# Vector c kept in place, rotated keys in common buffers, column sums at other rates, squares on VectorE in a one-core decoder block

## The chip, the cores and the metric

The kernel runs on one core of a Trainium2 chip. A core has TensorE (matmuls), VectorE, ScalarE and GpSimd, and SyncE, whose queue here only issues DMAs. In the profile they are called PE (and PEld for its weight loads), DVE, ACT, POOL and SP. The metric is the device time of one execution in microseconds; lower is better.

## The reference

One layer of a decoder on a sequence of 512 tokens, in float32, width 2048. All of it is conditioned on one vector `c`:

```python
c_act = silu(c)
sh_a, sc_a, gt_a, sh_f, sc_f, gt_f = split(c_act @ w_ada + b_ada, 6)
h = rmsnorm(x, norm_mix) * (1 + sc_a) + sh_a
p = h @ w_in            # c_q, c_kv, k_pe, q, k, v, z, b, a, gate logits
y_a = mla(c_q, c_kv, k_pe) @ w_o_mla      # 8 heads, causal softmax, rotary part of 64
y_b = gated_delta_net(q, k, v, z, b, a) @ w_o_gdn
g_a, g_b = split(sigmoid(gate_logits), 2)
x = x + gt_a * ((g_a * y_a + g_b * y_b) @ w_o)
h = rmsnorm(x, norm_ffn) * (1 + sc_f) + sh_f
gate, up = split(h @ w_gate_up, 2)
x = x + gt_f * ((silu(gate) * up) @ w_down)
return rmsnorm(x, final_norm)
```

The two places that the change touches are the product `c_act @ w_ada` (six chunks of 2048 columns) and, in `rmsnorm(x, norm_ffn)`, the sum of the squares of `x` over the 2048 features of each token. The rotary keys `k_pe` after their rotation are the third thing that is moved.

## The kernel before

**Matmuls.** Every large product is taken in three matmuls: an operand is split into a rounded part `hi` (a cast on ScalarE) and a remainder `lo` (a subtraction on VectorE, both in `halves`, lines 263 and 264, or in `hilo`, lines 239 and 240), and hi·hi, hi·lo and lo·hi are added in PSUM.

**Order of the work.** A `Unit` is one piece of a weight matrix: `load` issues its DMA on SyncE, `split` makes `hi` and `lo`, `mms` is its list of matmuls (24 for most), and `pre` and `post` run before and after them. The `Driver` keeps up to `LOADS` = 4 units loaded and `AHEAD` = 2 units split ahead of TensorE. After every `GROUP` = 12 matmuls it takes one step of each side chain (`pump`); the chains are Python generators that write out the delta net, the attention, the normalisations and so on, a few instructions to a step. The scheduler of the framework then orders each engine's instructions; those of SyncE, GpSimd and TensorE stay in the order of the program (`PINNED`), as do single instructions that are marked, column sums among them.

**Main units.** `mixing()` yields them in this order, numbered here by their index in `mixed`: one that loads scalars (0), `ga8` and `ga12` (1 to 16), the sets `q03`, `k03`, `v03` (to 40), `kb` (to 44), `gb0`, `gb1` (to 60), `q47` (to 68), `k47` (to 76), `v47` (to 84), `z0`, `cq`, `ckv`, `z1` (to 116), six units for the rotary queries and the values (to 122), the eight heads' `qk` (to 130), `gb2` and `gb3` (16 each, to 162: eight units with matmuls, and between them eight that only reload pieces of the normalised input, `hh` and `hl`, or copy `x`), `ya` (to 182), `yb` (to 202). Then come `wo0` to `wo2` in a Strassen scheme and `wo3` in two halves of 256 tokens. The head, before them, runs `s1` and takes the column sums of chunk 1. The attention is a side chain that runs beside `qk`, `gb2` and `gb3`: at step i it takes the values of tile i-3, the transposes of i-2, the softmax of i-1 and the scores of i.

**Extra units.** `mixed` slips units of a second list, `extras()`, between the main units: `plan(i)` of them after main unit i. They have no matmuls. In `mod_units` one of them loads 512 KB of `w_ada` and takes a column sum on VectorE (`mod_sum`, line 435): the product with `silu(c)`, spread over all partitions as the tile `cbc`, and its sum in one instruction. A chunk has 32 of them. In `ada_units` one loads 512 KB of `w_in` and adds two scaled rows into `acc`. The order of the list is: chunk 0, 3, 2, 4 (`gt_mix`), four times eight `ada_units`, chunk 5 (`gt_ffn`).

**Buffers.** The pool `slots` has 68 common buffers of 128 x 512; `raws` has five of 512 KB for loaded weights, main units' and column sums' alike; the pool `wides` has a single one of 1 MB. The last holds `cbc` first, then `kp`, the rotated keys' `hi` and `lo` (of which it uses half), then `cbc` again, read back from `c_dram` once the attention has ended, and at last `euvw` of the Strassen stages.

**Squares.** `squares(q, seg, eng)` takes the squares of one tile on ScalarE and adds them to a running sum on the engine `eng`. For `q` 4 to 7 that is VectorE; for `q` 0 to 3 they are added on GpSimd in the chain `wo_rest`, which also fetches these tiles back from `x2_dram` and the pieces `a21` for the second half of `wo3`. `part_rstd` sums over the features with the matmuls `hss`; `spread` makes `hbc`, the inverse root spread over the partitions; `h2_gen(h)` then makes the normalised input of the feed-forward part (`h2f`, `h2T`) for one half of the tokens. `gu0` and `gu1` consume it.

Of the kernel before, what the change touches and what calls it, by code (L numbers as in the profile page):

```python
# [8 lines left out]
F32 = mybir.dt.float32  # L9
# [162 lines left out]
def block_kernel(ctx: ExitStack, tc: tile.TileContext, a: dict, out, out_t):  # L172
# [26 lines left out]
    def load(dst, src):  # L199
        nc.sync.dma_start(dst, src)  # L200
# [200 lines left out]

    c_dram = dram.tile([1, 4, 512], F32, name="c_dram")
    cbc = []

    def spread_c_again():
        cbc[0] = wides.tile([P, 4, 512], F32, tag="wide", name="cbc2")
        load(cbc[0][:].rearrange("p j n -> p (j n)"), c_dram.rearrange("o j n -> o (j n)").partition_broadcast(P))


    def spread_c():
        cbc.append(wides.tile([P, 4, 512], F32, tag="wide", name="cbc"))
        row = S("crow")
        load(row[0:P:32, :], a["c"].rearrange("o (j n) -> (o j) n", j=4))
        for j in range(4):
            ps = PS("cb")
            r = slice(32 * j, 32 * j + 1)
            mm(ps[:], ones[r, :], row[r, :], start=True, stop=True)
            nc.scalar.activation(cbc[0][:, j, :], ps[:], AF.Silu)  # L420
        side(c_dram, cbc[0][0:1])

# [584 lines left out]
    def rope_tables():  # L1009
        invf, posi = C("invf", [P, 32]), C("posi", [P, NT], I32)  # L1010
        side(invf[:], a["inv_freq"].partition_broadcast(P).rearrange("p o h -> p (o h)"))
        side(posi[:], a["positions"].rearrange("o (t p) -> p (o t)", p=P))
        yield 2
        posf = C("posf", [P, NT])
        nc.vector.tensor_copy(posf[:], posi[:])
        tmp = S("rt")[:].rearrange("p (a t e) -> p a t e", a=4, t=NT)
        ang, n, t1, t2 = (tmp[:, i] for i in range(4))
        for t in range(NT):
            nc.vector.tensor_scalar(ang[:, t, :], invf[:], posf[:, t:t + 1], None, op0=ALU.mult)
        nc.vector.tensor_scalar(n[:], ang[:], 0.15915494309189535, None, op0=ALU.mult)  # L1020
        nc.vector.tensor_scalar(n[:], n[:], 12582912.0, -12582912.0, op0=ALU.add, op1=ALU.add)
        for part in (6.28125, 0.0019350051879882812, 3.019916050195388e-07, 2.3999e-13):
            nc.vector.scalar_tensor_tensor(ang[:], n[:], -part, ang[:], op0=ALU.mult, op1=ALU.add)
        lim = 3.1415925
        nc.vector.tensor_scalar(ang[:], ang[:], lim, -lim, op0=ALU.min, op1=ALU.max)
        nc.scalar.activation(sin_[:], ang[:], AF.Sin)
        nc.scalar.activation(cos_[:], ang[:], AF.Sin, scale=0.5)
        nc.vector.tensor_tensor(cos_[:], cos_[:], cos_[:], ALU.mult)
        nc.vector.tensor_scalar(cos_[:], cos_[:], -2.0, 1.0, op0=ALU.mult, op1=ALU.add)
        kr = S("kr")[:].rearrange("p (t e) -> p t e", t=NT)  # L1030
        yield 2
        rope(kr[:, :, 0:64], kpe[:], NT, sin_[:], cos_[:], (t1, t2))
        nc.scalar.copy(kr[:, :, 64:128], kr[:, :, 0:64])
        yield 14
        kp = wides.tile([P, 4, 512], F32R, tag="wide", name="kp")
        ps = PS("kpT")
        for t in range(NT):
            nc.tensor.transpose(ps[:, tok(t)], kr[:, t, :], ident)
        hi, lo = (kp[:, i, :] for i in range(2))
        nc.scalar.copy(hi, ps[:])  # L1040
        nc.vector.tensor_tensor(lo, ps[:], hi.bitcast(F32), ALU.subtract)
        kpT.extend((hi, lo))

    w_uq, w_ukv = a["w_uq"][0], a["w_ukv"][0]
# [97 lines left out]
    def attention():  # L1142
        items = [(h, qb) for h in range(8) for qb in range(4)]
        n = len(items)
        box = [dict() for _ in items]
        yps = {}

        def scores(i):
            h, qb = items[i]
            N = max(qb + 1, 2) * P  # L1150
            ps = PS("sc")
            for q, k in ((0, 0), (0, 1), (1, 0)):
                mm(ps[:, 0:N], QN[h][q][:, tok(qb)], KN[h][k][:, 0:N], start=q == k, stop=False)
            for k in range(2):
                mm(ps[:, 0:N], qpT[h][:, tok(qb)], kpT[k][:, 0:N], start=False, stop=k == 1)
            box[i]["ps"] = ps
            if qb == 3:
                del QN[h], KN[h]

        def softmax(i):  # L1160
            h, qb = items[i]
            N = (qb + 1) * P
            ps = box[i].pop("ps")
            m, s, r = (sm[:, i, j:j + 1] for j in range(3))
            nc.vector.tensor_tensor(ps[:, tok(qb)], ps[:, tok(qb)], neg, ALU.add)
            nc.vector.tensor_reduce(m, ps[:, 0:N], AX.X, ALU.max)
            nc.vector.tensor_scalar(m, m, -scale, None, op0=ALU.mult)
            p = S("P")
            nc.scalar.activation(p[:, 0:N], ps[:, 0:N], AF.Exp, bias=m, scale=scale, accum_out=s)
            nc.vector.reciprocal(r, s)  # L1170
            nc.vector.tensor_scalar(p[:, 0:N], p[:, 0:N], r, None, op0=ALU.mult)
            box[i]["p"] = p

        def transposes(i):
            h, qb = items[i]
            N = (qb + 1) * P
            p = box[i].pop("p")
            ps = PS("pT")
            for kb in range(qb + 1):
                nc.tensor.transpose(ps[:, tok(kb)], p[:, tok(kb)], ident)  # L1180
            s = S("pT")
            (nc.scalar.copy if i % 2 else nc.vector.tensor_copy)(s[:, 0:N], ps[:, 0:N])
            box[i]["pT"] = s

        def values(i):
            h, qb = items[i]
            s = box[i].pop("pT")
            if qb == 0:
                yps[h] = PS("yT")
            for kb in range(qb + 1):  # L1190
                mm(yps[h][:, tok(qb)], V[h // 4][kb][:, tok(h % 4)], s[:, tok(kb)], start=kb == 0, stop=kb == qb)
            if qb == 3:
                yT[h] = hilo(yps.pop(h)[:], "y")
                if h % 4 == 3:
                    del V[h // 4]

        for i in range(n + 3):
            if i < n:
                while items[i][0] not in QN or items[i][0] not in qpT:
                    yield  # L1200
                if i == 0:
                    yield 2
            if i >= 3:
                values(i - 3)
            if 2 <= i < n + 2:
                transposes(i - 2)
            if 1 <= i < n + 1:
                softmax(i - 1)
            if i < n:
                scores(i)  # L1210
            yield
# [99 lines left out]
    def strassen_wo(n):  # L1311
# [20 lines left out]
        def freed(i):  # L1332
            if n == 2:
                wo_x["x56"][i] = wo_x["x73"][i] = None
                if i == 5:
                    for q in (4, 5):
# [4 lines left out]
                        [(c, i, j, lambda k, c=c: [wo_part(c, k, xi) for xi in range(2)]) for c, i, j in PRODUCTS],  # L1341
                        wo_ready, outputs, freed)

    def wo_rest():

        def squared(h):
            for q in range(4):
                squares(q, HALF[h], nc.gpsimd)
                yield

        for h in range(2):
            for q in range(4):
                x2[h][q] = S("x2")
                side(x2[h][q][:], x2_dram[h, q])
                yield
            if h == 0:
                for n in range(4):
                    t = S("a21")
                    load(t[:], a21_dram[n])
                    if n % 2:  # L1360
                        yield
                    a21[n] = t
                yield from squared(0)
                for n in range(4):
                    a21[n] = hilo(a21[n][:], "a21")
                    yield
        yield from squared(1)

    oT = [None] * 8

# [132 lines left out]
    def extras():  # L1503
# [29 lines left out]
        yield from mod_units(3, lambda ks: mod_columns(s_ffn, ks, b_cols[:, SC_F // P:SC_F // P + 16], n_ffn))  # L1533

        yield from mod_units(2, lambda ks: mod_columns(sh_ffn, ks, b_cols[:, SH_F // P:SH_F // P + 16]))
        yield from gate_units(4, gt_mix, GT_A)
        for n in range(4):
            yield from ada_units(w_in, sh_mix, O_GA + 512 * n, cols_done(n))
        while "att" not in chains or chains["att"] in drv.chains:
            yield Unit()  # L1540
        yield act(spread_c_again)
        yield from gate_units(5, gt_ffn, GT_F)

    known = set()

    def plan(i):
        return 2.0 if i < 16 else 0.85 if i < 48 else 1.2

    def act(fn):
        return Unit(load=fn)  # L1550
# [46 lines left out]
    def mixing():  # L1597
# [106 lines left out]
            chains["rest"] = drv.add(wo_rest())  # L1704
        with_pre(first, last)

        def rest():
            drv.finish(chains["rest"])
        yield from first + with_pre(with_pre(second, start_h2(0)), rest)


    def half_of(tile_, k):
# [488 lines left out]
    def ffn():  # L2201
        def gu0():
# [18 lines left out]
            def start():  # L2221
                for c in wo_x:
                    wo_x[c][:] = [None] * 8
                a21[:] = [None] * 4
                start_h2(1)()
            with_pre(us[0], start)
            return us[0] + us[1]
# [276 lines left out]
```

## Time and profile before

| | |
|---|---|
| median of 3 runs | 2752.79 us (2750.74 to 2755.06) |
| profiled execution | 2757.86 us |
| its span in the trace | 2756.1 us |
| TensorE, matmuls | busy 2716.6 us (99%) |
| TensorE, weight loads | busy 2357.8 us (86%) |
| VectorE | busy 2101.9 us (76%) |
| ScalarE | busy 1206.6 us (44%) |
| GpSimd | busy 273.8 us (10%) |
| DMA | 563.25 MB, 204 GB/s on average |
| granted clock of TensorE | 0.995 on average |

The profiled execution is one run apart from the three timed ones. The span is what the trace covers; the device time holds 1.8 us more around it. All matmuls stand under line 155, the call behind which the wrapper hides every TensorE and GpSimd instruction, so they are told apart by the names of their tiles. A matmul's busy time overlaps that of the next, because they are pipelined.

### The profile page before, as it was taken

To read this page: it belongs to the slowest core of one execution; us is meant where nothing else is said; L and a number is where in the kernel's file an instruction comes from. 1 tells how busy PE (TensorE), PEld (TensorE's weight loads), DVE (VectorE), ACT (ScalarE), POOL (GpSimd) and SP (SyncE) were. 2 spreads that over 40 slices of the span, in tenths; PEclk is the share of its full clock that TensorE was granted. 3 is DMA by queue.
4 is the path that set the end of the run, shared out by engine and by line. 5 is a ranking of instruction groups with operands and counts; after the bars stand their busy time and mean duration, and the time that the engine had idled before them with its cause. 6 is when DMAs were issued, how large, how long until landed. Compare 5 with 4: busy or idle time off the path is not lost.

```text
span 2756.1 us, 41080 instructions
## 1 busy us (share of the span) xinstructions
PE 2716.6 (99%) x15292; PEld 2357.8 (86%) x15292; DVE 2101.9 (76%) x3348; ACT 1206.6 (44%) x1715; POOL 273.8 (10%) x370
## 2 busy tenths in 40 slices
PE   9999999999999999999999999999999999999998
PEld 7888788788888888889999888888888888998997
DVE  8786666777887556788787877778778777878866
ACT  3443432442254343234473444444444445446545
POOL 0000011102001000001200000000000103113113
PEclk9999999999999999999999999999999999999999
DMA  9897566656675638725764556665665668568565
GB/s 361 302 350 268 182 195 194 214 162 212 202 213 184 209 132 303 264 76 132 263 184 141 194 200 199 202 218 199 203 202 194 218 202 196 122 196 203 131 184 168
DMA packets 315520, 563.25 MB, mean 204 GB/s; under 512 B 40788, under 2 KB 120820, under 8 KB 315192
## 3 DMA queue, kind: packets, MB, share of 16 engines
q1 hardware_dynamic: 264776, 460.04, 50.9%
q0 software_dynamic: 31904, 74.77, 10.6%
q10 hardware_dynamic: 18640, 25.83, 2.6%
q8 instruction: 119, 1.95, 0.3%
q14 instruction: 81, 0.66, 0.1%
HBM read 477.67 MB, written 83.90 MB: 204 GB/s over the span
## 4 chain that ended last, share of the span: by engine, by line
PE 83%; DVE 7%; DMA 5%; issue 2%; ACT 2%; SPq 0%; ACTq 0%; POOL 0%; DVEq 0%; POOLq 0%
PE m L155 41%; PE gb L155 6%; PE v L155 4%; PE gu L155 3%; PE ya L155 3%; PE dn L155 3%; PE yb L155 3%; PE s L155 3%; PE z L155 3%; DMA raw<-in_w_in_dram 2%; PE k L155 2%; PE q L155 2%; PE wo L155 1%; DVE rawm L435 1%; PE qk L155 1%
## 5 line engine op out<-in xcount | busy, mean ns | idle before, releaser
L263 ACT CAST hi<-raw 128x1024 fp32r<-128x1024 f32 x250 | 259.7, 1040 | 560.3 <-DMA raw<-in_w_in_dram 220.4
L264 DVE TENSOR_TENSOR lo<-raw,hi 128x1024 fp32r<-128x1024 f32 x250 | 305.4, 1223 | 198.5 <-ACT hi L263 181.1
L1831 ACT CAST hi<-raws 128x512 fp32r<-128x512 f32 (+1 forms) x240 | 218.6, 911 | 327.5 <-PE m L155 264.0
L1832 DVE TENSOR_TENSOR lo<-raws,hi 128x512 fp32r<-128x512 f32 (+1 forms) x240 | 247.4, 1042 | 87.8 <-ACT hi L1831 87.6
L155 PE MATMUL m<-xl,hi 128*128 128x256 f32 x1088 | 309.7, 285 | 3.9 <-DVE xl L240 3.9
L155 PE MATMUL m<-xh,hi 128*128 128x256 f32 x1088 | 309.5, 284 | 3.9 <-ACT xh L239 2.3
L155 PE MATMUL m<-xh,lo 128*128 128x256 f32 x1088 | 309.4, 284 | 1.3 <-DVE lo L2007 1.3
L435 DVE CUSTOM_DVE_ANT_0 rawm<-rawm,cbc 128x1024 f32<-128x1024 f32 x192 | 234.2, 1237 | 8.6 <-DMA rawm<-in_w_mod_dram 8.3
L155 PEld LDWEIGHTS m<-xl,hi 128*128 128x128 f32 x1088 | 210.3, 193 | 4.8 <-DVE xl L240 4.7
L155 PEld LDWEIGHTS m<-xh,hi 128*128 128x128 f32 x1088 | 210.2, 193 | 4.6 <-ACT xh L239 2.7
L155 PEld LDWEIGHTS m<-xh,lo 128*128 128x128 f32 x1088 | 210.2, 193 | 1.7 <-DVE lo L2007 1.7
L155 PE MATMUL m<-hi,h2h 128*128 128x512 f32 x480 | 190.2, 396 | 0.4 <-DVE euvw L1849 0.4
L155 PE MATMUL m<-hi,h2l 128*128 128x512 f32 x480 | 187.2, 390 | 0.0
L155 PE MATMUL m<-lo,h2h 128*128 128x512 f32 x480 | 187.1, 390 | 0.0
L2006 ACT CAST hi<-sums 128x1024 fp32r<-128x1024 f32 x88 | 92.2, 1048 | 138.6 <-PE m L155 99.0
L2007 DVE TENSOR_TENSOR lo<-sums,hi 128x1024 fp32r<-128x1024 f32 x88 | 107.5, 1221 | 47.3 <-ACT hi L2006 47.2
L1831 ACT CAST hi<-sums 128x1024 fp32r<-128x1024 f32 x80 | 84.2, 1053 | 110.5 <-PE m L155 105.6
L1832 DVE TENSOR_TENSOR lo<-sums,hi 128x1024 fp32r<-128x1024 f32 x80 | 97.7, 1221 | 28.0 <-ACT hi L1831 27.6
L155 PEld LDWEIGHTS m<-hi,h2h 128*128 128x128 f32 x480 | 90.2, 188 | 19.1 <-DVE euvw L1849 1.5
L155 PEld LDWEIGHTS m<-hi,h2l 128*128 128x128 f32 x480 | 90.1, 188 | 18.9
L155 PEld LDWEIGHTS m<-lo,h2h 128*128 128x128 f32 x480 | 90.3, 188 | 17.5
L2006 ACT CAST hi<-raws 128x768 fp32r<-128x768 f32 x88 | 73.4, 835 | 69.6 <-PE m L155 47.4
(576 smaller groups left out, 7429.4 us busy)
## 6 DMA issues: line engine op xcount, KB each, us to landing
raws<-in_w_gate_up_dram SPq DMA_DIRECT2D x400, 256.0 KB, 3.6
rawm<-in_w_mod_dram SPq DMA_DIRECT2D x192, 512.0 KB, 5.2
raw<-in_w_in_dram SPq DMA_DIRECT2D x144, 512.0 KB, 4.9
raws<-in_w_down_dram SPq DMA_DIRECT2D x128, 256.0 KB, 4.1
s_dram<-raws POOLq DMA_DIRECT2D x80, 256.0 KB, 2.3
raws<-s_dram SPq DMA_DIRECT2D x80, 256.0 KB, 3.0
rawa<-in_w_in_dram SPq DMA_DIRECT2D x32, 512.0 KB, 4.7
raws<-in_w_o_dram SPq DMA_DIRECT2D x48, 256.0 KB, 3.1
```

Of the source, the lines that this page charges most:

```text
L155: return self.tc.keep_in_program_order(f(*args, **kwargs))
L263: nc.scalar.copy(hi[:], raw[:])
L264: (lo_eng or nc.vector).tensor_tensor(lo[:], raw[:], hi[:].bitcast(F32), ALU.subtract)
L435: r = nc.vector.tensor_tensor_reduce(raw, raw, c, 1.0, 0.0, ALU.mult, ALU.add, parts[:, k, half:half + 1])
L1831: nc.scalar.copy(hi[:], src)
L1832: nc.vector.tensor_tensor(lo[:], src, hi[:].bitcast(F32), ALU.subtract)
L2006: nc.scalar.copy(hi[:], src)
L2007: nc.vector.tensor_tensor(lo[:], src, hi[:].bitcast(F32), ALU.subtract)
```

## The change

- `spread_c_again` and the copy in `c_dram` go. `cbc` stays in the wide buffer until the last column sum, and the list of extras has no pause for the attention.
- The rotated keys are put in two of the common buffers, `kph` and `kpl`. `qpT[h]` is dropped after a head's last scores, `kpT` after the last head's.
- In `extras` the four `ada_units` blocks come ahead of chunk 4.
- `plan` gives other rates.
- In `wo_rest` the four tiles of a half are fetched back in one step, all eight adds of squares run on VectorE, and those of the second half wait until four tiles of `h2` of the first half are made. The second half of `wo3` waits only for the flag `rest[0]`; the chain itself is brought to its end at the start of `gu0`.

```diff
-    c_dram = dram.tile([1, 4, 512], F32, name="c_dram")
     cbc = []
-
-    def spread_c_again():
-        cbc[0] = wides.tile([P, 4, 512], F32, tag="wide", name="cbc2")
-        load(cbc[0][:].rearrange("p j n -> p (j n)"), c_dram.rearrange("o j n -> o (j n)").partition_broadcast(P))
-
...
             nc.scalar.activation(cbc[0][:, j, :], ps[:], AF.Silu)
-        side(c_dram, cbc[0][0:1])
...
-        kp = wides.tile([P, 4, 512], F32R, tag="wide", name="kp")
+        hi, lo = S("kph", F32R), S("kpl", F32R)
         ps = PS("kpT")
         for t in range(NT):
             nc.tensor.transpose(ps[:, tok(t)], kr[:, t, :], ident)
-        hi, lo = (kp[:, i, :] for i in range(2))
-        nc.scalar.copy(hi, ps[:])
-        nc.vector.tensor_tensor(lo, ps[:], hi.bitcast(F32), ALU.subtract)
+        nc.scalar.copy(hi[:], ps[:])
+        nc.vector.tensor_tensor(lo[:], ps[:], hi[:].bitcast(F32), ALU.subtract)
         kpT.extend((hi, lo))
...
             if qb == 3:
-                del QN[h], KN[h]
+                del QN[h], KN[h], qpT[h]
+                if h == 7:
+                    kpT.clear()
...
+    rest = [False]
+
     def wo_rest():
 
-        def squared(h):
-            for q in range(4):
-                squares(q, HALF[h], nc.gpsimd)
-                yield
-
-        for h in range(2):
+        def x2_back(h):
             for q in range(4):
                 x2[h][q] = S("x2")
                 side(x2[h][q][:], x2_dram[h, q])
-                yield
-            if h == 0:
-                for n in range(4):
-                    t = S("a21")
-                    load(t[:], a21_dram[n])
-                    if n % 2:
-                        yield
-                    a21[n] = t
-                yield from squared(0)
-                for n in range(4):
-                    a21[n] = hilo(a21[n][:], "a21")
-                    yield
-        yield from squared(1)
+
+        x2_back(0)
+        for n in range(4):
+            a21[n] = S("a21")
+            load(a21[n][:], a21_dram[n])
+            yield
+        for q in range(4):
+            squares(q, HALF[0], nc.vector)
+            yield
+        for n in range(4):
+            a21[n] = hilo(a21[n][:], "a21")
+            yield
+        x2_back(1)
+        rest[0] = True
+        while h2n[0] < 4:
+            yield
+        for q in range(4):
+            squares(q, HALF[1], nc.vector)
+            yield
...
-        yield from gate_units(4, gt_mix, GT_A)
         for n in range(4):
             yield from ada_units(w_in, sh_mix, O_GA + 512 * n, cols_done(n))
-        while "att" not in chains or chains["att"] in drv.chains:
-            yield Unit()
-        yield act(spread_c_again)
+        yield from gate_units(4, gt_mix, GT_A)
         yield from gate_units(5, gt_ffn, GT_F)
...
     def plan(i):
-        return 2.0 if i < 16 else 0.85 if i < 48 else 1.2
+        return 2.0 if i < 16 else 0.5 if i < 48 else 0.9 if i < 116 else 1.3 if i < 154 else 1.0
...
-        def rest():
-            drv.finish(chains["rest"])
-        yield from first + with_pre(with_pre(second, start_h2(0)), rest)
+        def ready():
+            while not rest[0]:
+                drv.step(chains["rest"])
+        yield from first + with_pre(with_pre(second, start_h2(0)), ready)
...
                 a21[:] = [None] * 4
+                need("rest")()
                 start_h2(1)()
```

## Rows read from the trace of the kernel before

**Rows 1.** The page, part 1: TensorE's busy time, share of the span, instructions.

```profile
PE 2716.6 (99%) x15292; PEld 2357.8 (86%) x15292; DVE 2101.9 (76%) x3348; ACT 1206.6 (44%) x1715; POOL 273.8 (10%) x370
```

**Rows 2.** TensorE's waits in all: for whom, us in total, times, longest.

```profile
PE k L155 <- DVE lo L264: 3.0, 1, 3.0
...
PE hss L155 <- DVE sq L1423: 2.7, 1, 2.7
...
PE pT L155 <- DVE sm L1167: 1.2, 1, 1.2
...
PE hbc L155 <- DVE diag L1446: 0.6, 1, 0.6
```

**Rows 3.** The table of stretches: start and end in us, length, busy time by engine.

```profile
core 0: us, PE busy (x) PEld busy (x) DVE busy (x) ACT busy (x) POOL busy (x), PEclk, DMA share, GB/s
...
11.00:99.00 88.00, 87.11 (x383) 71.90 (x384) 73.08 (x141) 31.24 (x40) 2.74 (x5) 1.00 0.97 355
...
430.00:1392.00 962.00, 950.71 (x5687) 825.98 (x5686) 720.86 (x1391) 389.16 (x625) 78.69 (x98) 0.99 0.61 197
...
511.00:513.00 2.00, 2.00 (x7) 1.52 (x6) 1.27 (x2) 0.00 (x0) 0.00 (x0) 0.50 0.92 336
...
877.00:915.00 38.00, 35.91 (x192) 30.62 (x191) 29.24 (x86) 12.55 (x31) 0.00 (x0) 0.96 0.68 235
...
895.00:958.00 63.00, 62.92 (x343) 54.60 (x342) 38.05 (x105) 22.45 (x51) 0.00 (x0) 0.97 0.62 201
915.00:978.00 63.00, 62.92 (x358) 55.07 (x357) 33.60 (x93) 22.71 (x51) 0.00 (x0) 1.00 0.53 175
1040.00:1085.00 45.00, 45.00 (x200) 37.27 (x199) 33.03 (x49) 15.97 (x20) 0.00 (x0) 1.00 0.91 315
```

**Rows 4.** TensorE's timeline in the stage of `k47`: start, duration, what, idle before.

```profile
505.62 0.39 PE L155 MATMUL k<-hl,hi 128*128 128x512 f32 x1
...
511.26 0.63 PE L155 MATMUL k<-hh,hi 128*128 128x512 f32 x1
```

**Rows 5.** VectorE's timeline in the same stage.

```profile
499.54 4.05 DVE L515 SCALAR_TENSOR_TENSOR cv<-cp,columns,cv 128x509 f32<-128x509 f32 x6
...
506.59 1.22 DVE L435 CUSTOM_DVE_ANT_0 rawm<-rawm,cbc 128x1024 f32<-128x1024 f32 x1
...
507.74 1.22 DVE L264 TENSOR_TENSOR lo<-raw,hi 128x1024 fp32r<-128x1024 f32 x1
```

**Rows 6.** The page, parts 5 and 6: column sums (mean ns); weight loads (us to landing).

```profile
L435 DVE CUSTOM_DVE_ANT_0 rawm<-rawm,cbc 128x1024 f32<-128x1024 f32 x192 | 234.2, 1237 | 8.6 <-DMA rawm<-in_w_mod_dram 8.3
...
raw<-in_w_in_dram SPq DMA_DIRECT2D x144, 512.0 KB, 4.9
```

**Rows 7.** VectorE's groups by line, 915 to 978 us.

```profile
L264 DVE TENSOR_TENSOR lo<-raw,hi 128x1024 fp32r<-128x1024 f32 x9 | 11.0, 1220 | 6.0 <-ACT hi L263 6.0
```

**Rows 8.** SyncE's timeline, 893 to 1012 us: when each DMA is issued.

```profile
950.25 0.32 SPq L155 DMA_DIRECT2D hl<-hspill  x1
950.62 7.71 SPq L155 DMA_DIRECT2D raw<-in_w_in_dram  x6
...
978.11 0.37 SPq L155 DMA_DIRECT2D raw<-in_w_in_dram  x1
1007.89 0.34 SPq L155 DMA_DIRECT2D cbc<-c_dram  x1
```

**Rows 9.** GpSimd's timeline in `wo3`.

```profile
1355.48 6.52 POOL L155 TENSOR_TENSOR sq<-sq,sq 128x512 f32<-128x512 f32 x4 [39.79 <-ACT sq L1421]
```

**Rows 10.** VectorE's timeline in `wo3`.

```profile
1357.44 5.10 DVE L240 TENSOR_TENSOR a21l<-a,a21h 128x512 fp32r<-128x512 f32 x3 [1.38 <-ACT a21h L239]
...
1363.61 0.68 DVE L240 TENSOR_TENSOR a21l<-a,a21h 128x512 fp32r<-128x512 f32 x1
1364.21 1.65 DVE L1411 SCALAR_TENSOR_TENSOR x<-wo,gt_mix,x 128x256 f32<-128x256 f32 x4
...
1371.96 2.31 DVE L264 TENSOR_TENSOR lo<-raw,hi 128x1024 fp32r<-128x1024 f32 x1
```

## The prediction

> **What bounds the kernel now.** I read the page first. TensorE is busy for 2716.6 us, 99% of the span [rows 1]: its matmuls set the time, and the change touches none of them. What can be won or lost is TensorE's idle time and the matmuls that run at the low clock. Next came the list of what TensorE waits for [rows 2]: nothing in it is long. The table of stretches gives a ceiling: between 430 and 1392 us, where nearly all of the change acts, TensorE is busy for 950.7 of 962.0 us [rows 3], so 11.3 us are idle. To this come matmuls at half clock after the longer waits. At 505 us, ahead of the wait of 3.0, a matmul takes 0.39 us; at 511, behind it, 0.63 [rows 4], and the granted clock from 511 to 513 is 0.50 [rows 3], the level of 1.2 GHz. Eight matmuls like that are 8 x 0.24 = 1.9 us. If each of the three waits over 1 us drags as much behind it, 11.3 + 3 x 1.9 = 17 us is all that the change could ever give back there, 0.6% of the time. About 0.2%, or 5.5 us, is what a measurement of this kernel can tell from no change.
>
> Then I followed the places one by one. In the stage of `k47` VectorE is late: six convolution steps (4.05 us) and column sums stand ahead of the `lo` split that TensorE needs, which starts only at 507.74 [rows 5]. In the attention the transposes `pT` wait for softmax steps on VectorE, and in `wo3` the matmuls `hss` wait 2.7 us for the last add of squares [rows 2].
>
> **Column sums at other rates.** The list of extra work stays the same, but for the second spread: 192 units, 160 of them column sums (the 32 of chunk 1 are taken in the head) and 32 of `ada_units`. A column sum is one VectorE instruction of 1.24 us [rows 6], 1.15 from start to start [rows 5], and one load of 512 KB. Only the places move. Counting the units of `mixing` in the order of the code, the 8 units of `k47` (and of each set like it up to `ckv`) carry 7.2 extras where they carried 9.6. `gb2` (units 131 to 146, its 8 reloads counted) carries 16 x 1.3 = 20.8 where it had none, because the second spread waited for the end of the attention: its load left at 1007.89 [rows 8], and the column sums behind it. `gb3` (147 to 162) carries 7 x 1.3 + 9 = 18.1. The gates `ya` and `yb` carry the remaining 24.4 at 1.0.
>
> In `k47` three column sums are left of four in the queue ahead of the late split: 1.15 us off 3.0 leaves 1.9, and some of the half clock. Bounds: nothing gained (the order of the queue is made anew, and the convolution steps remain), and the whole 3.0 + 1.9 = 4.9 us. I take -2.5, the middle, since VectorE also comes less loaded into the stage.
>
> In `gb2` the cost is new. VectorE is busy there for 33.6 of 63 us [rows 3], 11.0 of it with the splits [rows 7]; the softmax of 14 tiles is most of the rest. 20.8 x 1.15 = 23.9 us more makes 57.5 of 63, or 91%. There is room for that (VectorE is idle there for 29.4 us), so the lower bound is 0. But the softmax is a chain from TensorE to VectorE to ScalarE and back, and it must be through before the transposes two steps later. A column sum in front of a softmax step delays it by up to 1.15 us: 14 x 1.15 = 16.1 us if each tile paid it once in full. The steps are some 4.5 us apart (63 us for 14 tiles), which should absorb most of that. But between 877 and 915 us, where VectorE is busy for 29.2 of 38 us [rows 3], the same softmax did stall TensorE [rows 2]. I take +3.5, nearer to nothing than to 16, because the idle VectorE of this very stage is the nearest row.
>
> The loads add a second price. Between 895 and 958 us, when the loads for `gb2` are issued, 201 GB/s x 63 us = 12.7 MB move [rows 3]. 20.8 x 0.524 = 10.9 MB more makes 23.6 MB. The head, the fastest stage of this trace, moves 355 GB/s at a share of 0.97 [rows 3]: 66.4 us of transfers in 63 us. A backlog of 3.4 us is about what the loads' lead covers (the stage at 1040 has 315 GB/s and a share of 0.91 without any idle TensorE [rows 3]), so I take 0, bound +3.4. The Trainium skill speaks against the change here: its page "DMA: Bandwidth & Descriptors" (Specifications) puts the HBM limit of one core at about 358 GB/s, by which the same bytes would take an estimated 65.9 us. The trace agrees with that limit within 1%.
>
> **The spread c and the rotated keys.** The DMA to `c_dram` and the 1 MB load go, and with them a block of SyncE's queue from 978 to 1008 us [rows 8]. TensorE doesn't idle for it, since the weights of `gb3` had been issued by 978.11; worth 0 on the path. The keys take two of the 68 common buffers until the attention ends. The reloads of `hh` and `hl` are short of buffers already: one left at 950.25, and the weights queued behind it, six loads, from 950.62 on [rows 8]. The first of these belongs to the seventh unit of `gb2`, which starts at about 915 + 6 x 7.9 = 962. That leaves 11 us. Landing takes 4.9 of them [rows 6], and the copy to `hi` and the `lo` of 1.22 about 2.3, so some 4 us are cover. Two buffers less delay the reloads, and the weights behind them, by up to one step of the attention, 4.5 us. I take +0.5, bounds 0 and +4. Dropping `qpT[h]` and clearing `kpT` issue nothing: 0. The new order of `gate_units(4)` and `ada_units` has the same instructions, with `gt_mix` and `gt_ffn` complete in `gb3` and `yb`, before `wo0` asks for them: 0.
>
> **Squares and the second half.** GpSimd's eight adds go (the first four take 6.52 us [rows 9]), and VectorE gets eight of the same shape as an `a21l`, 0.68 us each [rows 10]: 5.4 us. While GpSimd adds, VectorE is slow: three `a21l` take 5.10 us where one alone takes 0.68, and a `lo` of 1.22 takes 2.31 [rows 10]. That is 3.1 + 1.1 = 4.2 us which VectorE gets back. The gated sums of the first half start behind those splits, at 1364.21 [rows 10], and `hss` waits for what follows. Without 3.1 us of lateness the wait of 2.7 shrinks to nothing, or to about 0.5 if the four new adds stand in the way, and the 0.6 at `hbc` [rows 2] goes. With half clock behind it 2.7 + 0.6 + 1.9 = 5.2 us are at stake; I take -3.3, bounds 0 (the new adds take exactly the place of the lateness) and -5.2. The second half's four adds, 2.7 us, come while `h2` is made for the first half, ahead of the splits for `gu0`, which run two units ahead of TensorE: 0, bound +2.
>
> **The sum.** -2.5 - 3.3 + 3.5 + 0.5 = -1.8 us; the ends are -10.1 and +25.5 (16.1 + 3.4 + 4 + 2). The profiled execution took 2757.86 us, 5.07 above the median of the runs shown, so the sum stands for 2756.1 there, and for **2751 us** beside the median of 2752.79: no change that can be told.
>
> **The rivals.**
> *All hidden, faster.* `gb2` absorbs its column sums in VectorE's idle 29 us, and the stalls of `k47` and `wo3` go with their half clock: -4.9 - 5.2 = -10.1, or 2743 us. For it: the stage at 1040 carries column sums at a full DMA queue without a stall [rows 3]. Against it: that stage has no softmax in it. Chance 0.30.
> *The attention becomes the bound, slower.* In `gb2` each tile's softmax pays one column sum: +16.1, less gains of 5.8, so 2763 us. It decides from the point where the delay on VectorE passes what lies between two steps, for instance when a column sum at the head of VectorE's queue waits for a load that stands in SyncE's queue behind a reload without a buffer; the softmax steps queued behind it then wait too. For it: 91% load, transfers at their limit, buffers short. Against it: VectorE has 29 us of room in this stage, and the load falls to 18.1 sums in `gb3`. Chance 0.22.
> *Nothing moves.* The instructions are put in another order, and the stalls of `k47` and `hss` stay or turn up elsewhere: 2753 us, chance 0.10.
> The forecast has 0.38.
>
> **How the numbers follow.** Faster by over 0.2% (under 2747.3): nearly all of the first rival and 0.06 of the forecast, 0.35. Slower (over 2758.3): 0.20 of the second, 0.05 from the forecast and the third, 0.25. Within: 0.40. The range reaches just past the first rival's price and to the second's, 2741 to 2763 us, beyond which I leave under 0.2; the forecast's own is 2746 to 2757.
>
> **What would show it.** Right: the wait of `k` for `lo` near 505 us under 2 us; `hss` under 1 us, no adds on GpSimd in `wo3`, `a21l` at 0.68; VectorE busy for about 57 of 63 us in `gb2` with a share of DMA near 1, and a few us of waits of `pT` or `yT` for softmax steps between 915 and 1010. Wrong: more than 10 us idle in `gb2`, or none; the stall of `k47` unchanged; new waits for `lo` at the start of `gu0`.

## The result: slower by a third of a per cent

The changed kernel takes 2764.86 us (median of 14 runs, 2759.05 to 2769.56); the kernel before, beside it on the same chips, 2754.53 (14 runs). The ratio is 1.0033, 95% interval 1.0023 to 1.0044: slower, by about 9 to 10 us. The forecast was "no change", 2751 us.

The profiled execution of after took 2764.43 us, its span 2762.5. The list of what TensorE waits for (us in total, times, longest) against [rows 2]: the wait of `k` is gone, `pT` has grown from 0.9 to 7.5, a new `yT` stands there, and `hss` has a second wait.

```profile
PE pT L155 <- DVE P L1165: 7.5, 8, 1.8
PE hss L155 <- DVE sq L1420: 3.9, 2, 3.1
...
PE yT L155 <- DVE pT L1176: 2.7, 1, 2.7
```

The table of stretches of after, columns as in [rows 3]:

```profile
478.00:524.00 46.00, 46.00 (x263) 37.98 (x262) 35.16 (x65) 21.64 (x33) 6.73 (x10) 1.00 0.67 218
...
877.00:914.00 37.00, 31.56 (x168) 26.64 (x166) 23.35 (x65) 13.50 (x31) 0.00 (x0) 0.95 0.70 236
914.00:978.00 64.00, 58.98 (x326) 50.75 (x326) 50.47 (x126) 17.86 (x42) 0.00 (x0) 1.00 0.82 275
...
911.00:913.00 2.00, 2.00 (x7) 1.52 (x6) 0.58 (x2) 1.90 (x5) 0.00 (x0) 0.50 1.00 374
1402.00:1406.00 4.00, 3.36 (x16) 3.39 (x17) 2.12 (x11) 1.56 (x3) 0.00 (x0) 0.50 0.63 209
```

TensorE, without idle time in the stage of `k47` now, idles 5.4 us between 877 and 914 and 5.0 in the next 64, where before it idled 2.1 and 0.1 us in stretches of the same work [rows 3]. The last two lines show the granted clock at 0.50, the level of 1.2 GHz, behind two of the waits.

Cut at the first matmul of each stage, the profiled executions give (us):

| stretch | before | after |
|---|---|---|
| start to `qk` | 838.5 | 832.3 |
| `qk` to `ya` (the attention) | 201.9 | 212.7 |
| `ya`, `yb`, the first three sets of `wo` | 298.8 | 298.8 |
| `wo3` | 52.6 | 48.4 |
| `gu0`, `gu1` | 93.5 | 99.5 |
| rest of the span | 1270.7 | 1270.8 |

In this pair of profiles, then, 10.4 us are won and 16.8 lost, in the attention and at `gu0`.

**How the attention loses them.** VectorE's timeline of after (start, duration, what, count, idle before and what ended it):

```profile
894.87 0.48 DVE L1165 TENSOR_SCALAR P<-P,sm 128x512 f32<-128x512 f32 x1
900.64 1.14 DVE L945 SCALAR_TENSOR_TENSOR sz<-oz,fo,sz 128x128 f32<-128x128 f32 x4 [5.29 <-DMA oz<-o_dram]
...
904.95 1.21 DVE L428 CUSTOM_DVE_ANT_0 rawm<-rawm,cbc 128x1024 f32<-128x1024 f32 x1
...
906.09 1.22 DVE L428 CUSTOM_DVE_ANT_0 rawm<-rawm,cbc 128x1024 f32<-128x1024 f32 x1
...
907.23 1.22 DVE L428 CUSTOM_DVE_ANT_0 rawm<-rawm,cbc 128x1024 f32<-128x1024 f32 x1
...
908.38 0.68 DVE L240 TENSOR_TENSOR yl<-yT,yh 128x512 fp32r<-128x512 f32 x1
...
908.98 0.28 DVE L1176 COPY pT<-pT 128x128 f32<-128x128 f32 x1
```

VectorE stands 5.29 us at the head of its queue, for a DMA (`oz`). What had gathered behind it follows in one piece: softmax steps, splits, three column sums, and last the copy `pT`. TensorE's timeline at that place, with the matmuls at 0.63 us behind the stall that take 0.39 elsewhere:

```profile
906.26 0.39 PE L155 MATMUL qk<-ckvh,lo 128*128 128x512 f32 x1
909.31 0.49 PE L155 MATMUL yT<-pT,V 128*128 128x128 f32 x2 [2.66 <-DVE pT L1176]
...
911.29 0.63 PE L155 MATMUL sc<-knl,qnh 128*128 128x512 f32 x1
```

This stall is 2.7 of the 12.2 us that TensorE waits in the attention (3.3 in before). And SyncE's queue meanwhile: it stands from 891.63 to 901.85 at a reload of `hh`, for most of this time because of `sz`, VectorE's work on `oz` (the last line, from SyncE's waits between 870 and 978 us). Then each load of weights waits for VectorE, and the one at 907.34 leaves when the second sum has ended. ScalarE had issued the `oz` that VectorE stands for at 893.96.

```profile
890.78 0.85 SPq L155 DMA_DIRECT2D rawm<-in_w_mod_dram  x1
901.85 0.33 SPq L155 DMA_DIRECT2D hh<-hspill  x1
...
904.46 2.07 SPq L155 DMA_DIRECT2D rawm<-in_w_mod_dram  x2
907.34 0.38 SPq L155 DMA_DIRECT2D raw<-in_w_in_dram  x1
...
893.96 0.33 ACTq L942 DMA_DIRECT2D oz<-o_dram  x1
...
SPq L155 <- DVE sz L945: 8.8, 1, 8.8
```

Bursts of three sums stand again at 915.6, 934.3 and 965.8, and `pT` waits another 1.8, 1.0, 1.2 and 0.8 us for softmax steps between 920 and 972.

**How `gu0` loses them.** ScalarE's, VectorE's and TensorE's timelines of after at 1399 us, and VectorE's and TensorE's of before in the same place:

```profile
1398.98 1.15 ACT L1418 ACTIVATE sq<-x 128x512 f32<-128x512 f32 x2
...
1399.68 1.22 DVE L264 TENSOR_TENSOR lo<-raw,hi 128x1024 fp32r<-128x1024 f32 x1
1400.82 0.68 DVE L1420 TENSOR_TENSOR sq<-sq,sq 128x512 f32<-128x512 f32 x1
1401.42 0.47 DVE L1731 SCALAR_TENSOR_TENSOR h2f<-x,s_ffn,hbc 128x256 f32<-128x256 f32 x1
1401.81 0.68 DVE L1420 TENSOR_TENSOR sq<-sq,sq 128x512 f32<-128x512 f32 x1
...
1402.64 1.84 PE L155 MATMUL hss<-ones,sq 128*128 128x1 f32 x8 [3.09 <-DVE sq L1420]
```

```profile
1396.48 0.68 DVE L1423 TENSOR_TENSOR sq<-sq,sq 128x512 f32<-128x512 f32 x1
...
1397.47 0.68 DVE L1423 TENSOR_TENSOR sq<-sq,sq 128x512 f32<-128x512 f32 x1
...
1399.11 0.95 PE L155 MATMUL hss<-ones,sq 128*128 128x1 f32 x8
```

`hss` of the second half stands in the same place of TensorE's queue in both kernels, behind the first 60 matmuls of `gu`, which take 7.4 us. What comes later in after are the last two squares: ScalarE starts them 6.8 us after the first matmul of `gu` (2.9 in before), behind a split and `h2`, and VectorE's adds of them start at 8.6 and 9.6 us (4.6 and 5.6 in before), behind two more. So `hss` waits 3.1 us, and the matmuls behind it run at half clock.

### The profile page after: what moved, and what is told of

The parts are those of the page before. It is cut to its first block, busy times and chain, and to the rows that moved or that the text cites. A ratio compares the mean times of both kernels' runs of the same rounds, so it can differ in the third digit from the quotient of the medians.

```text
span 2762.5 us, 41072 instructions
## 1 busy us (share of the span) xinstructions
PE 2718.1 (98%) x15292; PEld 2360.2 (85%) x15292; DVE 2098.2 (76%) x3356; ACT 1207.2 (44%) x1715; POOL 259.3 (9%) x361
## 3 DMA queue, kind: packets, MB, share of 16 engines
q0 software_dynamic: 31872, 74.76, 10.6%
## 4 chain that ended last, share of the span: by engine, by line
PE 90%; DVE 4%; DMA 2%; issue 1%; ACT 1%; SPq 0%; ACTq 0%; DVEq 0%; POOL 0%; POOLq 0%
PE m L155 42%; PE gb L155 5%; PE v L155 4%; PE gu L155 3%; PE z L155 3%; PE ya L155 3%; PE k L155 3%; PE dn L155 3%; PE q L155 3%; PE yb L155 3%; PE s L155 3%; PE ga L155 2%; PE wo L155 2%; PE ckv L155 2%; PE cq L155 2%
## 5 line engine op out<-in xcount | busy, mean ns | idle before, releaser
L263 ACT CAST hi<-raw 128x1024 fp32r<-128x1024 f32 (+1 forms) x250 | 259.9, 1041 | 541.5 <-DMA raw<-in_w_in_dram 125.8
L264 DVE TENSOR_TENSOR lo<-raw,hi 128x1024 fp32r<-128x1024 f32 (+1 forms) x250 | 304.0, 1217 | 229.1 <-ACT hi L263 219.3
L155 PEld LDWEIGHTS m<-xl,hi 128*128 128x128 f32 x1088 | 211.2, 194 | 4.7 <-DVE xl L240 4.7
L155 PEld LDWEIGHTS m<-xh,hi 128*128 128x128 f32 x1088 | 211.2, 194 | 4.3 <-ACT xh L239 2.7
L155 PEld LDWEIGHTS m<-xh,lo 128*128 128x128 f32 x1088 | 211.2, 194 | 2.3 <-DVE lo L2002 2.3
```

The source lines that it names most:

```text
L155: return self.tc.keep_in_program_order(f(*args, **kwargs))
L263: nc.scalar.copy(hi[:], raw[:])
L264: (lo_eng or nc.vector).tensor_tensor(lo[:], raw[:], hi[:].bitcast(F32), ALU.subtract)
```

## The experiments

Fourteen kernels, each timed beside the kernel before. Stage times are those of the table above, each from one profiled execution.

### Which part of the change

**e1_sums_only** is after with `wo_rest` and its start as before: sums, rates, order, `c` and keys of after, GpSimd's squares. **e2_squares_only** is before with the new `wo_rest` alone.

> The change without its last part: c kept, keys in common buffers, the new order and rates of the column sums, but the squares on GpSimd and the second half's timing as before. Theory: the loss has two places, the column sums that stand in VectorE's queue ahead of the softmax in gb2 and gb3 (qk and gb together 212.7 us in the trace of after, 202.0 before), and the late squares of the second half in gu0 (99.4 against 93.4). Then this kernel keeps the first alone, with the gain of 6 us up to qk and without the 4 us won in wo3: about 5 us over before, 2759 to 2760, with gu0 back at 93 us. Rival: the new rates are harmless and all of the loss is from the squares: 2754 or less.

> The kernel before with the last part of the change alone: all squares on VectorE, the second half's later. Theory: wo3 gains 4 us (no lateness on VectorE, hss under 1 us) and gu0 loses 6 (hss of the second half waits some 3 us and half clock follows), so +2 us, 2756; the attention stays at 202 us. Rival (squares are all of the loss): +9, 2763.

e1: 2763.75 us, 1.0024 (1.0015 to 1.0033); `qk` to `ya` 215.3, `wo3` 52.6, `gu` back at 93.5. e2: 2756.44, 0.9998 (0.9990 to 1.0007); `wo3` 50.1, `gu` 99.8. By its time e2 can't be told from before, so the squares give about what they take. (Its stages would make it +3.8 us, -2.5 and +6.3, where its interval ends at +1.9: single profiles are no better than that.) The loss of the kernel is in the part with the column sums. Its size in e1 was under-estimated.

### The squares: which place costs

**e5_no_delay** is after without the wait for the first half's `h2`; **e13_half_on_gpsimd** is before with the first half's adds alone on VectorE:

```diff
 e5, after:   -        while h2n[0] < 4:
              -            yield
 e13, before: -                squares(q, HALF[h], nc.gpsimd)
              +                squares(q, HALF[h], nc.gpsimd if h else nc.vector)
```

> The change as it is, but the second half's squares do not wait until four tiles of h2 are made: they are added on VectorE as soon as the tiles are back. Theory: the wait of hss in gu0 (3.1 us and the half clock behind it) goes, wo3 keeps most of its gain: 6 us less than the change, 2758 to 2759. Rival (the wait comes from the mere number of adds on VectorE): under 2 us less, or wo3 loses what gu0 gains.

> The kernel before with one edit: the four adds of squares of the first half on VectorE, those of the second half on GpSimd as before, nothing later. Theory A (the place of the second half's adds on VectorE made the loss): wo3 takes 48 to 50.5 us instead of 52.7, gu0 and gu1 stay at 93.5, the time is 2751 to 2754 us. Rival B (GpSimd's adds slow VectorE in wo3 whichever half they are of): wo3 stays at 52 to 53 and the time at 2755 to 2757.

e5: 2764.69, 1.0029 (1.0019 to 1.0038). `gu` is back at 93.4, but `wo3` takes 55.1: the wait has moved there whole. The expected 2758 to 2759 was wrong, its rival right. e13: 2752.27, 0.9988 (0.9979 to 0.9998); `wo3` 50.6, `gu` 93.5. TensorE's waits for `hss` in e5 and in e13:

```profile
PE hss L155 <- DVE sq L1418: 4.4, 1, 4.4
```

```profile
PE hss L155 <- DVE sq L1423: 0.9, 1, 0.9
```

So by these stages the first half's adds are well placed on VectorE, and the second half's are not, early or late; on GpSimd they harm nothing. e13's gain is small (its interval ends just under 1), and e14 below doesn't confirm it.

### The attention: the sums or their loads

**e7_sums_cut** lets the sums of chunks 4 and 5 add 64 of 1024 columns, **e8_loads_cut** leaves their loads out (the sums read `c` twice). The gates are then wrong or incomplete; nothing else is left out.

```diff
 e7: +        if few:
     +            raw, c = raw[:, 0:64], c[:, 0:64]
 e8: +        if chunk >= 4:
     +            return
              load(raw[:]..., w_mod[chunk, ...])
     -        ...tensor_tensor_reduce(raw, raw, c, ...)
     +        ...tensor_tensor_reduce(raw, c if own else raw, c, ...)
```

> The kernel after, but the column sums of chunks 4 and 5 add up only 64 of their 1024 columns (so gt_mix and gt_ffn are left incomplete); their loads stay as they are. These are nearly all the sums that after puts beside the attention. Theory Q (VectorE's queue: bursts of three sums of 1.15 us ahead of the softmax steps): the stretch from the first matmul of qk to the first of ya goes from 212.7 us back to about 203, the wait of 7.9 us behind the softmax at 906 goes, and the time is about 2755 us (after 2765). Rival D (the loads: transfers at their limit, buffers short): the stretch stays at 211 to 213 and the time at 2764.

> The kernel after, but the column sums of chunks 4 and 5 take the spread c twice instead of a weight tile, and their 64 loads of 512 KB are left out (gt_mix and gt_ffn are then no gates); the instructions on VectorE stay as long as they are. Theory Q (VectorE's queue): the stretch from qk to ya stays at 211 to 213 us and the time at 2763 to 2765. Rival D (loads): the stretch goes back to about 203 and the time to about 2755. Should both this and the cut sums come out in the middle, a sum at the head of the queue waits for its late load, and the two act together.

e7: 2755.25, 0.9993 (0.9985 to 1.0002); `qk` to `ya` 201.2. e8: 2754.78, 0.9992 (0.9983 to 1.0001); 203.6. Each alone takes away nearly all of the loss, so neither theory holds by itself: sums without loads cost 2 to 3 us in the attention, loads without long sums nothing, the two together 11 (12.5 in the mean of three profiles, below). One thing limits this: the scheduler makes VectorE's order anew for each kernel. Of some 400 VectorE instructions around the attention, about 90 stand elsewhere in e7 and in e8 than in after (in e1 and e5 none). That the other order helped, and not the cut alone, is not ruled out. The stretch 914 to 978 in e7 and in e8, and from VectorE's timeline of e8 the start of the first burst of three sums:

```profile
914.00:978.00 64.00, 62.93 (x354) 55.02 (x353) 35.10 (x131) 22.32 (x50) 0.00 (x0) 1.00 0.85 296
```

```profile
914.00:978.00 64.00, 61.67 (x345) 53.63 (x346) 50.16 (x129) 21.66 (x49) 0.00 (x0) 1.00 0.34 108
```

```profile
897.18 1.22 DVE L430 CUSTOM_DVE_ANT_0 rawm<-cbc 128x1024 f32<-128x1024 f32 x1
```

In e8 VectorE is as busy as in after (50.16 against 50.47) and has the same bursts of three, but this one starts 66.4 us behind the start of `qk`, in after 72.7; in e7 the DMA share is as high as in after (0.85 against 0.82). What differs, besides the order, is who waits for whom between 870 and 978 us. SyncE's waits for a column sum, and VectorE's for `oz`, in after, in e7, and in e8:

```profile
SPq L155 <- DVE parts L428: 22.6, 18, 5.5
...
DVE sz L945 <- DMA oz<-o_dram: 7.5, 2, 5.3
```

```profile
SPq L155 <- DVE parts L430: 7.5, 5, 3.2
...
DVE sz L947 <- DMA oz<-o_dram: 6.6, 3, 3.3
```

```profile
SPq L155 <- DVE parts L430: 8.3, 3, 5.9
...
DVE sz L947 <- DMA oz<-o_dram: 2.1, 2, 1.7
```

In after VectorE comes to `oz` 1.4 us after its issue and stands until it lands, its queue then runs in one piece, and SyncE, whose loads share the five `raw` buffers with the weights, waits 18 times for a sum to give one back. This repeats: the long wait for `oz` is 5.3, 5.5 and 5.4 us in after, e1 and e5. Without the loads VectorE does not stand long (2.1 us; in before 2.8); with them it does (7.5, 6.6), but without the long sums it catches up at once. That chain is read from the traces; no run took away the late `oz` alone, or gave the sums buffers of their own. That `oz` lands 6.7 us after its issue in after, 5.9 in e7 and 4.7 in e8. In before one takes 9.2 us, and VectorE comes to it later, so the transfer's own length doesn't explain the wait. The loads of the sums go out on SyncE's queue, the `oz` on ScalarE's: the Trainium skill states ("Trainium Kernel Development and Optimization", Key Constraints) that DMAs issued from these queues run on the same 16 DMA engines and interleave, and the landing times of after and e8 agree with it.

### Order, keys, the spread c, and few sums

**e3_pause_old_rates** is e1 with before's rates and none beside `gb2` and `gb3`; **e4_pause_old_order** is the same with before's order of `gate_units(4)` and `ada_units`, and with its pause from unit 134 on instead of 131; **e10_lean_attention** is e1 with other rates:

```diff
 e3:  +        return 2.0 if i < 16 else 0.85 if i < 48 else 1.2 if i < 131 else 0.0 if i < 163 else 1.2
 e4:  +        return 2.0 if i < 16 else 0.85 if i < 48 else 1.2 if i < 134 else 0.0 if i < 163 else 1.2
 e10: +        return 2.0 if i < 16 else 0.5 if i < 48 else 0.9 if i < 116 else 1.8 if i < 131 else 0.3 if i < 163 else 1.3
```

> As the first, but with the rates of before and no extra units in gb2 and gb3: c kept, keys in common buffers, no second spread. Theory (the column sums beside the softmax cost, not the two buffers): qk and gb together back at 202 us, the stall of k47 back at 3 us, and the time of before, 2754 within 3 us. Rival (the two common buffers that the keys take delay the reloads): qk and gb stay over 207 us and the time over 2758.

> The run with the pause in the attention (e3_pause_old_rates: before's rates, none beside the attention, squares as before) with before's order as well: the sums of chunk 4 ahead of the ada units. The c that stays and the keys in common buffers remain as in after. Theory O (the new order made the stalls of e3 at 506, 564 and 645 us): the stretch from the start to qk goes from 842.4 us back to about 838.5, and the time is 2755 to 2757, that of before. Rival K (the keys in common buffers, the c that stays): the stretch stays at 841 to 843 and the time at 2762 to 2764.

> The kernel after with squares as before, and fewer column sums beside the attention: after's rates up to 116, then 1.8 up to 131, 0.3 in gb2 and gb3 (10 units where after has 39), 1.3 in the gates. Theory QD (sums and loads together make the attention late; a sum every 25 us doesn't): k47 gains as in after, qk to ya 202 to 205 us, the time 2750 to 2753. Rival K (the keys' buffers cost 6 us whatever the rates): 2756 to 2759. Rival V (24 more units in the gates make a stall there): ya and yb over 182 us instead of 177.9.

e3: 2764.14, 1.0027 (1.0018 to 1.0037). e4: 2763.12, 1.0023 (1.0012 to 1.0034). e10: 2767.09, 1.0042 (1.0030 to 1.0054). None comes out as one of its theories said. e3 gives the attention its 202.4 back, but takes 842.4 to `qk`: with that order at these rates, TensorE waits at `cq` and `k`. e4 has the stretch to `qk` of its theory O (838.8) and the time of its rival K, because it loses in a place that neither looked at: 207.3 in the attention. e10 put nine sums, by its 1.8, between 840 and 914 us, where the softmax is at work too, and takes 214.4; another 4 us go from `ya` to `wo3`. Waits of TensorE up to `qk` in e3, then in the attention in e4 and in e10:

```profile
PE cq L155 <- DVE b_ga L1503: 2.5, 1, 2.5
PE k L155 <- DVE lo L264: 2.4, 1, 2.4
```

```profile
PE yT L155 <- DVE pT L1176: 3.9, 1, 3.9
```

```profile
PE pT L155 <- DVE P L1165: 8.0, 6, 2.0
PE yT L155 <- DVE pT L1176: 3.7, 4, 1.3
```

The wait in e4 is the one of after again, after two sums only (at 900.95 and 902.81): VectorE stands 3.44 us for the `hi` of a weight tile whose load left late, at 906.75, and the copy `pT` stands behind it. e10's expectation counted the sums ("a sum every 25 us"); these two runs suggest that where they stand, and what stands late ahead of them, counts more.

**e9_keys_only** is before with the rotated keys in two common buffers; **e12_keys_and_c** keeps the spread `c` as well (no `c_dram`, no second load).

> The kernel before with one edit: the rotated keys in two common buffers instead of a wide tile; rates, order, second spread and squares of before. Theory K (two common buffers less cost time all the way to the end of the attention; they are what the two runs with a pause in the attention, e3 and e4, still lose): 2761 to 2763 us. Rival W (the keys cost the 0.5 us of the prediction): 2755 to 2757 us.

> The run with the keys in common buffers (e9_keys_only), and the spread c kept in its tile: no DMA to c_dram, no second load of 1 MB; chunk 5 still waits for the end of the attention. Theory K: as with the keys alone, 2761 to 2763 us. Rival W: 2755 to 2757. If the keys alone cost nothing and this is at 2762, what e3 and e4 lost is in the c that stays or in the sums that follow on it.

e9: 2754.91, 0.9998 (0.9989 to 1.0007). e12: 2755.82, 0.9999 (0.9991 to 1.0008). Neither costs anything; theory K falls.

### A version that beats both

**e6_rates_at_k47** and **e11_rates_at_ckv** are before with other rates; **e14_best_and_half** is e11 with the edit of e13.

```diff
 e6:  +        return 2.0 if i < 16 else 0.85 if i < 48 else 1.3 if i < 68 else 0.5 if i < 78 else 1.3
 e11: +        return 2.0 if i < 16 else 0.85 if i < 48 else 1.3 if i < 68 else 0.5 if i < 78 else 1.6 if i < 100 else 0.8 if i < 112 else 1.5
```

> The kernel before with nothing but other rates: 1.3 instead of 1.2 a unit from q03 to q47, 0.5 in the ten units around k47, 1.3 behind them; the pause in the attention, the second spread, the keys' tile and the squares stay. It takes the prediction's first term alone. Theory G (the column sums ahead of the late lo were that stall): the k wait of 3.0 us at 505 goes, 2.5 to 5 us are gained, the time is 2751 to 2753. Rival M (the list is only shifted: what leaves k47 stalls q47, v47 or z0 instead): 2755 to 2757.

> The kernel before with other rates alone: as in e6_rates_at_k47, 0.5 a unit around k47, and 0.8 in the twelve units ahead of the transposes cT, where e6 met a wait of 3.2 us for ckv; 1.6 and 1.5 elsewhere. Theory G (each stall goes when the extras ahead of it go): start to qk 832 to 835 us, the time 2750 to 2752. Rival M (the extras only stall another place): 2755 to 2757.

> The fastest rates so far (e11_rates_at_ckv, 2749 us) with the same edit of the squares. Theory A: 2745 to 2747 us. Rival B: 2748 to 2750 us.

e6: 2756.90, 0.9998 (0.9990 to 1.0007): the wait at `k47` goes, and one of 3.2 us comes at 755, rival M. The line of e6:

```profile
PE cT L155 <- DVE ckv L980: 3.2, 1, 3.2
```

e11, which holds the extras back there as well: 2749.18, 0.9976 (0.9966 to 0.9986), start to `qk` 833.2, the attention 198.1. The wait at 755 is gone with that of `k47`. e14: 2747.09, 0.9975 (0.9963 to 0.9986), not to be told from e11. Both are faster than both kernels; between 840 and 978 us e11 has no sum, like before. Why its attention is some 3 us shorter than before's (198.0 in e6, too) isn't shown.

## Why the prediction was wrong, step by step

**The step that failed is "In `gb2` the cost is new", the term of +3.5, with the 0 for the loads beside it: the two were priced apart and added.** The attention from `qk` to `ya` lost 10.8 us in the one pair of profiles, and 12.5 in the mean of three each (before, e2, e13: 201.9, 200.2, 199.6; after, e1, e5: 212.7, 215.3, 211.2). The number of sums was nearly right (18 in 64 us, for 20.8 in 63), and the load of VectorE was lower than forecast (50.5 us, not 57.5). Taken alone, each price comes out: the sums without loads cost 2 to 3 us (e8), the loads without long sums nothing (e7). Together they cost 12.5, and the forecast had no term for that. (Two runs show this, and in both VectorE's order changed, too.)

The reason behind the low price was VectorE's idle time of 29.4 us as room. Some 16 us of it were filled, in after and, at little cost, in e8. But it was not free for any use. In before's profile VectorE's waits between 915 and 978 us are these:

```profile
DVE yl L240 <- ACT yh L239: 8.4, 3, 3.1
DVE lo L264 <- ACT hi L263: 6.0, 3, 2.6
DVE pT L1182 <- PE pT L155: 5.5, 3, 1.9
DVE sc L1165 <- PE sc L155: 5.1, 3, 2.7
DVE sm L1170 <- ACT P L1169: 4.8, 3, 2.0
```

So it is time that VectorE stands at the head of its queue, 19.2 us for ScalarE and 10.6 for TensorE, and none of it for a transfer. In after it also stands for `oz`, and what has gathered behind runs in one piece, with sums ahead of the steps that TensorE needs. The bound of 16.1 held.

**The rival "the attention becomes the bound" happened**, at 2764.9 us for its 2763. That the totals are so near is in part luck: it had +16.1 and gains of 5.8, and measured were +12.5, gains of 8.3 and a loss of 6.0 at `gu0` that it didn't have. Its cause was half right: a transfer stands at the head of VectorE's queue, with softmax steps behind it. But what VectorE waits for is `oz`, which comes by ScalarE's queue, the sums stand behind it, and the reload that stands in SyncE's queue waits for VectorE in its turn. Its condition, sum and late load together, agrees with e7 and e8.

**The second half's adds, taken as 0, bound +2, cost 6.0 us** (e2: 6.3). The prediction looked at the splits for `gu0`, which are not late. It overlooked that `hss` of the second half stands 60 matmuls into `gu0`, and that the last two squares and their adds would come 4 us later there. To the wait of 3.1 come 0.9 for the eight `hss` at half clock (1.84 for 0.95) and 2.0 for twenty matmuls of `gu` that start 0.21 us apart instead of 0.12.

**`wo3`, -3.3:** measured -4.3 (before, e9, e12: 52.6, 53.4, 52.6; after, e7, e8: 48.4, 48.7, 48.6). VectorE's timeline of after shows an `a21l` at 0.69 us, of which three took 5.10 beside GpSimd's adds [rows 10], and the new adds beside them:

```profile
1356.92 2.88 DVE L1420 TENSOR_TENSOR sq<-sq,sq 128x512 f32<-128x512 f32 x4
1359.72 0.69 DVE L240 TENSOR_TENSOR a21l<-a,a21h 128x512 fp32r<-128x512 f32 x1
```

The Trainium skill states ("Advanced Engine Details and Errata", GPSIMD Details) that GpSimd shares a read and a write interface to the on-chip memory (SBUF) with VectorE, and conflicts with VectorE's instructions that have two inputs there. The trace agrees: this subtraction has two such inputs, and takes 0.69 us against 1.70 beside GpSimd's adds.

**`k47`, -2.5:** the wait is gone as foreseen, and VectorE is busy for 35.2 of 46 us. But the 6.2 us that the pair of profiles gives up to `qk` are too many. Before, e2, e9 and e13 issue the same instructions in the same order on all engines there, and the wait measured 3.0, 2.1, 0.3 and 1.0 us, the stretch 838.5, 834.9, 833.1 and 835.4. Against their mean of 835.5, after and its kin (e1, e5, e7, e8 have the same start: 832.3, 832.8, 830.8, 830.9, 830.8) win 4.0 us. Of these, 2.3 lie between the starts of `gb0` and `z0`, where `k47` is, for the term's 2.5. The term was right, but by some luck: the row it came from was one execution's draw, the largest of the four.

**The rest.** DMA in `gb2`, 0: 275 GB/s at a share of 0.82 on average; in e7 the stretch moves 296 GB/s at no cost, so the bytes alone are not what costs. The Trainium skill's 358 GB/s ("DMA: Bandwidth & Descriptors", Specifications) is not a ceiling in these traces: before moves 407 GB/s from 11 to 21 us. The 355 GB/s that the prediction found within 1% of it is the mean of 88 us, and not the most that was moved. The spread `c` and the keys, +0.5: nothing (e12). The order of `ada_units`, 0: nothing at after's rates, where `cq` waits 0.9 us as before; at before's rates it made a wait of 2.5 (e3).

The sum with the measured terms is -4.0 + 12.5 - 4.3 + 6.0 = +10.2 us; the medians differ by 10.3. So close a match is luck: the terms come from profiles that scatter by 1 to 5 us, and e2's stages miss e2's time by some 2 us at least.

What is not settled: how much of the loss in the attention is the scheduler's order, how much the wait for `oz` and how much the shared buffers; and why e4 loses there with two sums only. The trace of e4 shows the late load and the queue behind it, but no run took that one load away.

## What to carry to other kernels

Idle time of an in-order engine is room only where work put there would not stand in front of something that TensorE waits for: look at what ended each idle time and at what is queued behind it, not at the share. Two small prices need not add: here extra work and its loads each cost 3 us or less alone and 12.5 together. So ask of a stage with a tight chain what late loads and extra work do to each other, the more so where that work shares its load buffers with the weights. Before a stall of one profile is taken as a gain, look at its size in a second execution.

## What was not expected of the hardware

The same instruction order gave waits of 0.3 to 3.0 us at one place in four executions, and the first of the two down stages that follow each other at 2311 us took 170.5 us in before's profile and 172.8 to 174.0 in after, e1, e2, e3 and e5, with the same waits in before and after (`m` for `xl`: 3.9 and 3.8). Behind them the granted clock is below full speed for one stretch of 10 us in before (0.83 from 2330 to 2340) and for three in after (0.66, 0.88 and 0.78 from 2340 to 2370). A difference of 2 to 3 us between two single profiles says little here; the medians of many runs say more.
